# Decay products padded from 64 to 128 rows, and a new matmul price in the planner, in a two-block fp32 model kernel

## The chip, the cores and the metric

The kernel runs on one core of one Trainium2 chip. The metric is device time in microseconds (us) of one execution; before the change the median of three runs is 2162.2 us (2161.71 to 2162.23).

## What is computed

The kernel carries 512 tokens of 1024 features, in float32, through two blocks. The first one has a short convolution mixer, a gated feed-forward layer, a sparse attention mixer with compressed keys, and a second feed-forward layer. The second one runs a state-space mixer (16 heads) and a stick-breaking attention mixer (16 heads) side by side, sums both through one output projection and ends with a feed-forward layer. The change touches the state-space mixer, of which this is what matters:

```python
a_cs = jnp.cumsum(a_dt, axis=-1)            # within chunks of 128 tokens, per head
seg = a_cs[..., :, None] - a_cs[..., None, :]
decay = jnp.exp(jnp.where(causal, seg, -jnp.inf))
scores = jnp.einsum("bclgn,bcsgn->bcgls", cm, bm)
y_diag = jnp.einsum("bcgls,bcgels,bcsgep->bclgep", scores, decay, xg)
...
y_off = jnp.einsum("bclgn,bcgepn,bcgel->bclgep", cm, prev_states, jnp.exp(a_cs))
```

## The kernel before, in words

Activations lie feature-major, 128 features by 512 tokens in a tile. A float32 operand is split into a high and a low part of the type fp32r (`hilo`, `split`), and a product is three matmuls, high by high, low by high, high by low (`mm3`), summed in a PSUM bank of 128 x 512. Weights stream from HBM in groups of eight 128 x 128 blocks (`raw`); ScalarE casts a group to its high part `wh`, VectorE subtracts to get `wl`, and two split groups are held at a time (`prep`, `blk`). Tiles are named by use in the profile: `d` is the PSUM tile of any projection, `xh`/`xl`, `hb`, `hidh`/`hidl`, `ysh`/`ysl` are split activations, `qk` the token-major queries, keys and values, `lg` and `bt` the logits and log weights of a stick-breaking head, `so` its output, `ks` its stacked keys.

The program is written in stages: `layer_a` (with its feed-forward), `nsa` (compression, sparse attention, feed-forward), `block2`. In `block2` and in `nsa` independent streams are interleaved by `weave`, each with a start and an end on a common scale.

None of this is issued at once. A `Recorder` takes down every instruction, prices it and lists what it depends on (`add`, `cost`, lines 240 to 270). `arrange` then runs a list scheduler over the whole program: `forward` (L327) gives each engine, at each step, the instruction that can start first by the planner's clock, ties going to the one whose latest start, found by `backward` (L295), is earliest; for VectorE, ScalarE and GpSimd a more urgent instruction that is ready a little later can go first. Transfers on SyncE's queue are taken by program order. Some instructions may run on one of several engines (`any`), and the scheduler picks one. The result is an order of instructions for each engine and a place for each tile; the hardware then runs each queue in that order, behind semaphores. `emit` (L478) issues them, so in the profile nearly every instruction has the line L485, and tiles tell them apart.

The planner's price of a TensorE instruction stands at lines 252 to 256:

```python
passes = 1 if ins[-1].dtype == F32R else 2 if method == "transpose" else 6
o.dur = size(outs[0]) * passes / 2.4 + 3.0
o.load = (int(ins[0].ap.shape[-1]) if method == "matmul" else 128) / 1.2
```

`o.load` is the least distance to the start of the product before it (`begin`, L378). A VectorE instruction on n columns costs n * 1.042 + 68 ns, with additions for a scalar per partition and a lower rate for plain copies (L262).

The decay product is in `weights`, inside `ssd_pair` (L1373 to L1385). `ssd_prep` (L1263) puts the transposed running sums of the 16 heads into `at`, 64 rows by 512 tokens: the high part in rows 0 to 15, the low part in rows 32 to 47, zeros elsewhere (L1329 to L1332). `er` (L741) is a 64 x 16 matrix of ones at rows h and 32 + h of column h, made in `setup` from the constants, whose rows 64 to 127 are zero (L82). For each head one matmul with column h of `er`, repeated 128 times, as its weights spreads the sum of that head over all 128 partitions (L1376):

```python
mm(al, self.er[:, hd:hd + 1].to_broadcast([64, 128]), self.at, start=True, stop=True)
```

From `al`, ScalarE takes an exponential (`e`) and VectorE four differences (`dec`), from which the decay matrix of the head follows. There are 8 pairs of heads and so 16 such matmuls; the matmuls around them in PE's queue belong to other streams and have 128 rows.

Of the kernel before, what the change touches and what calls it, by code (L numbers as in the profile page):

```python
# [6 lines left out]
F32R = mybir.dt.float32r  # L7
# [79 lines left out]
def weave(*streams):  # L87
    """emits instruction streams side by side: (generator, the total of what it yields, start, end)"""
    live = [[float(st[2] if len(st) > 2 else 0), i, st] for i, st in enumerate(streams)]
    while live:  # L90
        s = min(live)
        g, total = s[2][:2]
        a, b = s[2][2:] if len(s[2]) > 2 else (0.0, 1.0)
        try:
            s[0] += (b - a) * next(g) / total
        except StopIteration:
            live.remove(s)
# [12 lines left out]
class View:  # L110
    """an access pattern of a tile that gets its place when the instructions are ordered"""
# [21 lines left out]
class Slot:  # L133
    """one tile as the program sees it, from its first access to its last"""
# [21 lines left out]
class Recorder:  # L156
    """records the instructions of the program, orders those of every engine by the time at which their
    operands are there and by their place in the program, and gives the tiles their places"""
# [8 lines left out]
    # from the end on one engine to the start on another  # L167
# [27 lines left out]
    def any(self, *ways):  # L195
        """one instruction that several engines can do, the usual one first: (engine, method, arguments)"""
        for i, (eng, method, a, *k) in enumerate(ways):
            k = k[0] if k else {}
            if i == 0:
                self.add(eng, method, a, k)  # L200
                continue
            x = Op()
            x.eng, x.call = eng, (method, a, k)
            self.cost(x, method, a, k, [a[0]], [v for v in a[1:] if isinstance(v, View)])
            self.ops[-1].ways[eng] = x.dur, x.call
# [36 lines left out]
    def cost(self, o, method, a, k, outs, ins):  # L242
        """nanoseconds on the engine, and those of a transfer"""
        size = lambda v: int(np.prod(v.ap.shape[1:]))
        n = max([size(v) for v in ins + outs[:1]])
        psum = any(v.t.psum for v in ins)
        # a scalar per partition
        one = any(isinstance(x, View) and size(x) == 1 for x in (k.values() if o.eng == "scalar" else a[2:]))
        o.move = 0.0
        if "dma" in method:  # L250
            o.dur, o.move = 1038.0 if o.eng == "gpsimd" else 475.0, size((outs + ins)[0]) * 128 * 4 / 360.0
        elif o.eng == "tensor":
            passes = 1 if ins[-1].dtype == F32R else 2 if method == "transpose" else 6
            o.dur = size(outs[0]) * passes / 2.4 + 3.0
            # the next product waits until its own matrix is loaded
            o.load = (int(ins[0].ap.shape[-1]) if method == "matmul" else 128) / 1.2
        elif o.eng == "scalar":
            o.dur = n / 1.2 + (51 if psum else 93) + (93 if one else 0) + (93 if "accum_out" in k else 0)
            o.tab = self.TABLES.get(a[2]) if method == "activation" else None
        elif o.eng == "vector":  # L260
            fast = not psum and method in ("tensor_copy", "tensor_scalar")
            o.dur = n * (6.26 if method == "reciprocal" else 0.52 if fast else 1.042) + 68 + (61 if one else 0)  # L262
        else:
            o.dur = n / 1.2 + 36
            if method == "affine_select":
                o.dur = n * 1.91
            elif method != "memset":
                o.dur = n / 1.2 + 160 + (84 if one else 0) + (n * 1.25 if method == "tensor_tensor" else 0)

    def place(self, ap):  # L270
        """the pattern on the place its tile got"""
        if not isinstance(ap, View):
            return ap
        t = ap.t
        home = t.real if t.real is not None else self.make(t, t.place)
        x = bass.AP(home.tensor, ap.ap.offset, ap.ap.ap)
        return x if x.dtype == ap.dtype else x.bitcast(ap.dtype)
# [17 lines left out]
    def backward(self):  # L295
        """the latest starts, from the end of the program"""
# [30 lines left out]
    def forward(self, urgent, look, timed=False):  # L327
# [26 lines left out]
        def avail(t):  # L354
            """when the tile can have a place, or None"""
# [15 lines left out]
        def begin(e, i, limit):  # L371
            """when the engine can start the instruction, or None if not by the limit"""
# [14 lines left out]
            if e in other:  # L387
                # one engine at a time reads a bank
                for t in o.banks:
                    at = max(at, t.read.get(other[e], -1e9) + self.LAG[other[e]][e])  # L390
            if e != o.eng:
                # another engine has to be done with it earlier than the usual one
# [8 lines left out]
        while first < len(ops):  # L401
            best = None
            for e, lst in cand.items():
# [10 lines left out]
                if top is not None and timed and e in self.PATIENT:  # L414
                    # a more urgent one that is ready soon goes first if that makes the later of the two less late
# [74 lines left out]
class Body:  # L490
# [26 lines left out]
    def alike(*views):  # L517
        """whether the Pool engine can do it: in SBUF, on the same partitions, of a size that is worth it"""
# [22 lines left out]
    def copy(self, out, a, scale=None):  # L541
        """a, by a factor"""
# [21 lines left out]
    def load(self, g, parts=None):  # L564
        """starts the transfer of a group of weight blocks"""
# [59 lines left out]
    def dense_g(self, name, n, x, ks=None, m=128):  # L625
        """the same as dense, in steps"""
# [7 lines left out]
    def dense_seq(self, specs, x, ks=None, first=2, late=1):  # L634
        """yields the finished PSUM tile of every (name, n); the late operands are used last in the first tiles,
        or every operand in all of them before the next one"""
# [10 lines left out]
    def dense_halves(self, specs, x, ks=None):  # L647
        """the same for the halves of the tokens, the first halves of all tiles before the second ones"""
# [12 lines left out]
    def dense_late(self, specs, x, first):  # L661
        """dense_seq where the second halves of the tokens come later: the first tiles take them last"""
        out = [self.ps("d") for _ in range(first)]
        for h, sl in enumerate(HALVES):
            for (name, n), p in zip(specs, out):
                # one accumulation group per bank: its first write clears the bank's flags
                self.half(p[:, sl], name, n, x, range(len(x)), sl, h == 0, h == 1)
# [5 lines left out]
    def rsq(self, src, scale, eps):  # L673
        """rsqrt(scale * src + eps) by logarithm and exponential, and a step of Newton"""
# [10 lines left out]
    def allsum(self, acc):  # L685
        """the sums over the partitions, on all of them"""
# [35 lines left out]
    def setup(self):  # L722
# [18 lines left out]
        self.er = self.nc.tile([64, 16], F32R, "er")  # L741
        nc.vector.tensor_copy(self.er, self.cst[0:64, C_E:C_E + 16])
# [71 lines left out]
    def ffn(self, x, rinv, name, gate, after, ada=False, early=0, late=0):  # L814
        """early: the first tiles take the second halves of the tokens last; late: the last tiles in halves"""
# [34 lines left out]
    def dense_out(self, name, x, late, ks=None, **kw):  # L850
        """the tiles of a product with the residual's rows, the last ones in halves: (n, PSUM, columns)"""
# [10 lines left out]
    def nsa(self):  # L862
# [39 lines left out]
        # gates token-major  # L902
# [50 lines left out]
    def stack(self, r, par, name="qs"):  # L953
        """[hi; lo] of one half of the rows, hi in its own rows"""
# [63 lines left out]
    def nsa_group(self, g):  # L1018
        """operands of one group of heads: stacked queries, doubled keys, distances, compressed values"""
# [143 lines left out]
    def block2(self):  # L1163
        nc = self.nc
        self.cols2()
        # final norm of the first block and the first norm of the second
        hb = [[self.pg(F32R, "hb") for _ in range(2)] for _ in range(ND)]
        for sl in HALVES:
            ss = self.allsum(self.acc[:, sl])
            q = self.allsum(self.acc2[:, sl])  # L1170
            # r1 * rsqrt(r1^2 q / D + e2) = rsqrt(q / D + e2 / r1^2)
# [53 lines left out]
    def share(self, name, ys, half):  # L1225
        """what half of the rows of the output projection add"""
# [7 lines left out]
    def cols2(self):  # L1234
        """per-feature factors of the two modulated norms"""
# [15 lines left out]
    def conv(self, p, j, u):  # L1251
        """causal depthwise convolution and bias of one tile of xBC"""
# [10 lines left out]
    def ssd_prep(self, hb):  # L1263
# [33 lines left out]
        # softplus: max(x, 0) + log(1 + e), e = exp(-|x|), the logarithm corrected for the rounding of 1 + e  # L1297
# [31 lines left out]
        self.at = self.pg(F32R, "at")[0:64]  # L1329
# [24 lines left out]
    def ssd_pair(self, i):  # L1354
# [18 lines left out]
        def weights(h):  # L1373
            hd = 2 * i + h
            al = self.ps("al")
            mm(al, self.er[:, hd:hd + 1].to_broadcast([64, 128]), self.at, start=True, stop=True)  # L1376
# [21 lines left out]
        # states at the end of the chunks  # L1398
# [39 lines left out]
    def sb_qk(self, nm, i, hb):  # L1438
        """queries, keys (normed over each head) or values of two pairs of heads, token-major"""
        nc = self.nc  # L1440
        p = [self.ps("qk") for _ in range(2)]
        for k in range(ND):
            w = self.blk(nm, k, i, n=2)
            for t in range(4):
                o = p[t // 2][:, 256 * (t % 2):256 * (t % 2) + 256]
                x = [y[:, 128 * t:128 * t + 128] for y in hb[k]]
                # one accumulation group per bank: its first write clears the bank's flags
# [10 lines left out]
    def sb_qk2(self, hb):  # L1458
        """the same for the first two pairs, the first halves of the tokens of queries and keys before the second ones"""
# [69 lines left out]
    # one head of the stick-breaking mixer: key tile -> (unit, column), as [keys, queries]  # L1529
# [11 lines left out]
    def sb_logits(self, hd):  # L1541
        """softplus of the logits where the key lies before the query, in two parts"""
# [16 lines left out]
    def sb_out(self, hd):  # L1559
# [12 lines left out]
        for u in (2, 0, 1):  # L1572
            w = sum(n for _, _, n in self.UNITS[u])
            b = self.ps("bt")
            # log weight: logit - (sum of the softplus terms from this key to the query)
# [28 lines left out]
    def strict(self, ap):  # L1604
        """keeps the entries whose key lies before the query"""
# [4 lines left out]
def _prepare(inputs):  # L1610
    """lays the inputs out: one matrix per name of the block stream, one array of per-partition columns"""
# [96 lines left out]
```

## Time and profile before

| | |
|---|---|
| median of 3 runs | 2162.2 us |
| span of the profiled execution, first to last instruction | 2159.8 us |
| TensorE products (PE) | 2117.5 us busy, 98% of the span, 11113 products |
| weight loads (PEld, beside PE) | 1789.1 us, 83% |
| VectorE (DVE) | 1386.1 us, 64% |
| ScalarE (ACT) | 941.8 us, 44% |
| GpSimd (POOL) | 425.9 us, 20% |
| HBM traffic | 98 GB/s over the span |

The profiled execution's own time is not listed apart from the three runs; its span is 2159.8 us, 2.4 us below their median, and that difference lies ahead of the first and behind the last instruction.

How to read it: the span runs from the first to the last instruction. A row of the timeline gives the start in us, the duration in us, engine, line, operation, the tile that is written and those that are read, and after x how many equal instructions are merged; in brackets stands the idle time of the engine ahead of it and what ended it. Records of successive matmuls overlap, since they are pipelined, so the time that a matmul takes from PE is the distance to the start of the next. The granted clock (PEclk) is 1.00 for 2.4 GHz and 0.50 for 1.2 GHz.

### The profile page before, as it was taken

Reading aid. Unit: us, or ns where it says so; the run is one execution under the profiler, and the core shown is the slowest. Engines: PE = TensorE matmul, PEld = TensorE weight load, DVE = VectorE, ACT = ScalarE, POOL = GpSimd, SP = SyncE. Lnnn points to the kernel's source line nnn. Section 1 sums busy time; section 2 is a strip of 40 time slices with the busy share of each in tenths; the row PEclk is TensorE's granted clock in tenths of the full one; section 3 lists DMA queues with packets and bytes.
Section 4 is the critical chain, followed back from the end, with each engine's and each line's share of the span. In section 5 each row is a group of like instructions: output and inputs, shape, how many; then the busy total and the mean of one; then the engine's idle time right before and its main releaser. Section 6 shows DMA issues by size and latency. Waiting matters only on the chain.

```text
span 2159.8 us, 28829 instructions
## 1 busy us (share of the span) xinstructions
PE 2117.5 (98%) x11113; PEld 1789.1 (83%) x11113; DVE 1386.1 (64%) x2347; ACT 941.8 (44%) x1587; POOL 425.9 (20%) x558
## 2 busy tenths in 40 slices
PE   8999999999999999999999999999999998999999
PEld 7888888888788777888888887989897888888887
DVE  6578754644868996654355598787879867333333
ACT  4233322332335885322222477677667746222221
POOL 1023320211223763000000141221315222000000
PEclk9999999999999999999999999999999999999999
DMA  4245652533332000222222332111121124222222
GB/s 166 98 178 188 212 183 97 175 117 104 104 127 72 1 1 31 97 98 98 98 98 98 117 127 79 59 50 59 59 69 40 40 95 140 98 98 98 98 98 98
DMA packets 60682, 214.04 MB, mean 99 GB/s; under 512 B 7424, under 2 KB 7552, under 8 KB 60544
## 3 DMA queue, kind: packets, MB, share of 16 engines
q1 hardware_dynamic: 52704, 186.50, 24.9%
q0 software_dynamic: 7840, 25.70, 3.5%
q8 instruction: 87, 1.43, 0.3%
q14 instruction: 51, 0.42, 0.1%
HBM read 210.07 MB, written 2.10 MB: 98 GB/s over the span
## 4 chain that ended last, share of the span: by engine, by line
PE 86%; DVE 9%; ACT 2%; issue 2%; POOL 1%; DMA 0%; SPq 0%; DVEq 0%; ACTq 0%; POOLq 0%
PE d L485 71%; PE qk L485 5%; PE bt L485 2%; PE o L485 2%; DVE wl L485 1%; PE so L485 1%; PE pt L485 1%; PE s L485 1%; DVE pr L485 1%; PE lg L485 1%; DVE e L485 1%; DVE ptl L485 1%; ACT wh L485 1%; DVE ss L485 0%; PE chid L485 0%
## 5 line engine op out<-in xcount | busy, mean ns | idle before, releaser
L485 ACT CAST wh<-raw 128x1024 fp32r<-128x1024 f32 (+1 forms) x332 | 347.6, 1048 | 873.1 <-PE d L485 736.8
L485 DVE TENSOR_TENSOR wl<-raw,wh 128x1024 fp32r<-128x1024 f32 (+1 forms) x342 | 424.6, 1242 | 417.3 <-ACT wh L485 414.5
L485 PE MATMUL d<-xh,wh 128*128 128x512 f32 (+1 forms) x1064 | 417.4, 394 | 6.0 <-ACT xh L485 6.0
L485 PE MATMUL d<-xh,wl 128*128 128x512 f32 (+1 forms) x1064 | 416.5, 392 | 1.0 <-DVE wl L485 1.0
L485 PE MATMUL d<-xl,wh 128*128 128x512 f32 x1064 | 416.3, 391 | 0.0
L485 PE MATMUL d<-hb,wh 128*128 128x512 f32 (+1 forms) x1136 | 332.7, 377 | 3.6 <-ACT hb L485 3.3
L485 PEld LDWEIGHTS d<-xh,wh 128*128 128x128 f32 (+1 forms) x1064 | 200.5, 189 | 47.6 <-ACT xh L485 6.0
L485 PEld LDWEIGHTS d<-hb,wh 128*128 128x128 f32 x1136 | 205.5, 190 | 40.1 <-ACT hb L485 3.5
L485 PEld LDWEIGHTS d<-xh,wl 128*128 128x128 f32 (+1 forms) x1064 | 200.3, 188 | 43.7 <-DVE wl L485 1.8
L485 PEld LDWEIGHTS d<-xl,wh 128*128 128x128 f32 x1064 | 200.4, 188 | 41.6 <-issue 0.7
L485 PE MATMUL d<-hb,wl 128*128 128x512 f32 (+2 forms) x568 | 212.3, 376 | 2.5 <-DVE wl L485 2.5
L485 PE MATMUL d<-hidh,wl 128*128 128x512 f32 (+1 forms) x561 | 211.8, 378 | 0.0
L485 PE MATMUL d<-hidh,wh 128*128 128x512 f32 (+1 forms) x561 | 211.5, 377 | 0.0
L485 PE MATMUL d<-hidl,wh 128*128 128x512 f32 (+1 forms) x561 | 211.5, 377 | 0.0
L485 PE MATMUL qk<-wh,hb 128*128 128x256 f32 x768 | 145.0, 288 | 2.1 <-ACT hb L485 1.0
L485 POOL TENSOR_TENSOR acc<-acc,sq 128x512 f32<-128x512 f32 (+1 forms) x24 | 38.2, 1591 | 499.7 <-ACT sq L485 441.9
L485 PEld LDWEIGHTS qk<-wh,hb 128*128 128x128 f32 x768 | 121.8, 193 | 6.5 <-DVE hb L485 1.5
L485 PEld LDWEIGHTS d<-hb,wl 128*128 128x128 f32 (+1 forms) x568 | 107.3, 190 | 22.6 <-DVE wl L485 3.5
L485 PEld LDWEIGHTS d<-hidl,wh 128*128 128x128 f32 x561 | 105.6, 188 | 19.4
L485 PEld LDWEIGHTS d<-hidh,wh 128*128 128x128 f32 x561 | 105.6, 188 | 19.3
L485 PEld LDWEIGHTS d<-hidh,wl 128*128 128x128 f32 x561 | 105.6, 188 | 19.2
L485 PE MATMUL qk<-wl,hb 128*128 128x256 f32 x384 | 109.0, 286 | 1.5 <-DVE wl L485 1.5
(370 smaller groups left out, 3678.5 us busy)
## 6 DMA issues: line engine op xcount, KB each, us to landing
raw<-in_wall_dram SPq DMA_DIRECT2D x345, 512.0 KB, 3.2
ada<-in_wada_dram POOLq DMA_DIRECT2D x96, 256.0 KB, 4.6
res<-in_x_dram SPq DMA_DIRECT2D x8, 256.0 KB, 7.3
out_dram<-res SPq DMA_DIRECT2D x8, 256.0 KB, 2.0
raw<-in_wall_dram SPq DMA_DIRECT2D x2, 256.0 KB, 3.7
cond<-in_c_dram POOLq DMA_DIRECT2D x2, 256.0 KB, 5.3
cst<-in_consts_dram SPq DMA_DIRECT2D x1, 394.5 KB, 7.0
mst<-in_consts_dram SPq DMA_DIRECT2D x1, 320.0 KB, 3.8
```

Source lines behind the costliest of these rows:

```text
L485: r = getattr(getattr(self.real, o.eng), m)(*[self.place(x) for x in a], **{n: self.place(x) for n, x in k.items()})
```

## The change

Two edits change what runs. The decay product gets 128 rows: `er` and `at` have 128 rows, the added ones zero. And the planner's price of a TensorE instruction changes from columns/2.4 + 3 ns to columns x 17/16/2.4 + 1 ns, with 3 ns more in the distance that a weight load imposes. No other constant of the planner and none of the weave's is changed. Everything else in the diff takes out docstrings and comments.

```diff
@@ class Recorder @@
     MARGIN = 704.3
-    # from the end on one engine to the start on another
+    COLUMN = 17 / 16 / 2.4
+
     LAG = {
@@ def cost @@
         elif o.eng == "tensor":
             passes = 1 if ins[-1].dtype == F32R else 2 if method == "transpose" else 6
-            o.dur = size(outs[0]) * passes / 2.4 + 3.0
-            # the next product waits until its own matrix is loaded
-            o.load = (int(ins[0].ap.shape[-1]) if method == "matmul" else 128) / 1.2
+            o.dur = size(outs[0]) * passes * self.COLUMN + 1.0
+
+            o.load = (int(ins[0].ap.shape[-1]) if method == "matmul" else 128) / 1.2 + 3.0
@@ def setup @@
-        self.er = self.nc.tile([64, 16], F32R, "er")
-        nc.vector.tensor_copy(self.er, self.cst[0:64, C_E:C_E + 16])
+        self.er = self.nc.tile([128, 16], F32R, "er")
+        nc.vector.tensor_copy(self.er, self.cst[:, C_E:C_E + 16])
@@ def ssd_prep @@
-        self.at = self.pg(F32R, "at")[0:64]
+        self.at = self.pg(F32R, "at")
         nc.vector.memset(self.at.bitcast(F32), 0.0)
@@ def weights, in ssd_pair @@
-            mm(al, self.er[:, hd:hd + 1].to_broadcast([64, 128]), self.at, start=True, stop=True)
+            mm(al, self.er[:, hd:hd + 1].to_broadcast([128, 128]), self.at, start=True, stop=True)
```

## Rows read from the trace of the kernel before

**Rows 1.** The page: span, and busy time of each engine.

```profile
span 2159.8 us, 28829 instructions
...
PE 2117.5 (98%) x11113; PEld 1789.1 (83%) x11113; DVE 1386.1 (64%) x2347; ACT 941.8 (44%) x1587; POOL 425.9 (20%) x558
```

**Rows 2.** Windows by stage: length, each engine's busy us (products), clock, DMA share, GB/s.

```profile
40.00:560.00 520.00, 520.00 (x2292) 430.13 (x2292) 310.42 (x479) 148.06 (x173) 108.11 (x139) 1.00 0.42 147
560.00:600.00 40.00, 34.99 (x168) 28.79 (x167) 38.58 (x51) 15.54 (x19) 15.53 (x12) 0.96 0.36 120
...
680.00:840.00 160.00, 153.92 (x1041) 124.05 (x1040) 151.18 (x504) 131.75 (x401) 101.92 (x161) 1.00 0.02 8
...
1320.00:1760.00 440.00, 431.79 (x2908) 385.35 (x2906) 354.15 (x585) 307.90 (x528) 120.28 (x155) 1.00 0.17 57
```

**Rows 3.** The page's groups: ScalarE's weight casts and the idle time ahead of them.

```profile
L485 ACT CAST wh<-raw 128x1024 fp32r<-128x1024 f32 (+1 forms) x332 | 347.6, 1048 | 873.1 <-PE d L485 736.8
```

**Rows 4.** Window of a dense stretch, instructions of tile d alone.

```profile
100.00:500.00 400.00, 399.70 (x1763) 330.69 (x1762) 48.16 (x70) 0.00 (x0) 1.00 0.47 162
```

**Rows 5.** Timeline of PE around one decay product.

```profile
1421.10 0.40 PE L485 MATMUL d<-hb,wl 128*128 128x512 f32 x1
1421.42 0.49 PE L485 MATMUL al<-at,er 64*128 64x512 f32 x1
1421.85 0.44 PE L485 MATMUL lg<-qh,ks 128*128 128x384 f32 x1
1422.12 0.34 PE L485 MATMUL lg<-ql,ks 128*128 128x384 f32 x1
1422.30 0.23 PE L485 MATMUL lg<-qh,ks 128*128 128x128 f32 x1
```

**Rows 6.** Timeline of the weight loads at the same place.

```profile
1421.42 0.18 PEld L485 LDWEIGHTS al<-at,er 64*128 64x128 f32 x1 [0.36 <-DVE wl L485]
1421.84 0.19 PEld L485 LDWEIGHTS lg<-qh,ks 128*128 128x128 f32 x1 [0.24 <-issue]
```

**Rows 7.** Timeline of PE around the sparse attention's gate transposes.

```profile
641.48 0.40 PE L485 MATMUL d<-xh,wh 128*128 128x512 f32 x1
641.81 0.46 PE L485 MATMUL gt<-cst,gr 64*128 64x64 f32 x4
642.20 0.49 PE L485 MATMUL d<-xl,wh 128*128 128x512 f32 x1
642.53 0.39 PE L485 MATMUL d<-xh,wl 128*128 128x512 f32 x1
```

**Rows 8.** Tile al: ns least/median/most, first and last start, form.

```profile
L485 PE MATMUL al<-at,er x16: 491/497/498, 1334.9 to 1697.1; 64*128 64x512 f32 x16
```

**Rows 9.** Tile at: its memset.

```profile
L485 DVE MEMSET at<- x1: 485/485/485, 1266.4 to 1266.4; 64x512 f32 x1
```

**Rows 10.** Timeline of PE in a stretch of 256-column products.

```profile
1810.47 0.40 PE L485 MATMUL d<-hb,wh 128*128 128x256 f32 x2
1810.71 0.28 PE L485 MATMUL d<-hb,wl 128*128 128x256 f32 x1
```

**Rows 11.** Timeline of DVE, two equal instructions and the next one.

```profile
562.50 1.29 DVE L485 TENSOR_TENSOR cx<-craw,vecs 128x512 f32<-128x512 f32 x2
563.70 1.63 DVE L485 TENSOR_TENSOR wl<-raw,wh 128x1024 fp32r<-128x1024 f32 x1
```

**Rows 12.** Timeline of the weight loads: the longest wait of the woven stage.

```profile
1653.26 0.19 PEld L485 LDWEIGHTS bt<-qh,ks 128*128 128x128 f32 x1 [2.41 <-DVE ks L485]
```

**Rows 13.** Timeline of DVE during that wait.

```profile
1649.96 1.46 DVE L485 CAST pvh<-pv 128x384 fp32r<-128x384 f32 x1
1651.46 0.96 DVE L485 TENSOR_TENSOR pvl<-pv,pvh 128x384 fp32r<-128x384 f32 x1
1652.45 0.76 DVE L485 SCALAR_TENSOR_TENSOR ks<-tq,vecs,ks 64x512 fp32r<-64x512 f32 x1
```

**Rows 14.** Windows of that wait and of the stretch behind it.

```profile
1650.50:1659.20 8.70, 4.95 (x36) 4.09 (x34) 8.50 (x12) 4.66 (x9) 5.67 (x6) 1.00 0.16 62
1659.20:1662.60 3.40, 3.14 (x8) 2.58 (x9) 3.37 (x7) 2.70 (x6) 0.59 (x1) 0.50 0.00 0
```

## The prediction, made before the changed kernel was run

> **What bounds the kernel now.** I read the page's busy times first: the tensor engine (PE) works in 2117.5 of 2159.8 us [rows 1]. A time is therefore changed by what PE is handed, by how fast it takes it, or by its 42.3 us of idle time, and by nothing else for long. Then I split the span by stage [rows 2]. The reader is to see two kinds of stage. In the feed-forward and projection stretches (40 to 560 us is the longest) PE is busy 520.00 of 520.00 us, while VectorE (DVE) has 310 us of work. The weight casts wait for PE and not the other way round: ScalarE sat idle for 873.1 us in front of them, 736.8 of it until a product was done [rows 3]. The mixed stages have gaps: PE idles 5.0 us in 560 to 600 (compression), 6.1 us in 680 to 840 (the sparse attention, where DVE is busy 151.2 of 160 us) and 8.2 us in 1320 to 1760 (state space and stick-breaking woven together). That is 19.3 of the 42.3 us; the rest lies at both ends of the program and in two handovers around 1250 and 1785 us, where a norm must be finished before a projection can begin. Third, I read single products: what does one cost in its place?
>
> **Part one: 128 rows in place of 64 in the decay product.** Busy time hides the answer, since records overlap; the distance from one start to the next is the price. In 100 to 500 us the `d` products alone number 1763 in 400 us [rows 4], so a 512-column product costs 400/1763 = 0.227 us. Around one decay product `al` [rows 5] the starts are 1421.10, 1421.42, 1421.85, 1422.12, 1422.30. The product ahead of it takes 0.32 instead of 0.227, the decay product 0.43 instead of 0.227, the 384-column one behind it 0.27 instead of the 0.18 of its twin. The sum is 0.09 + 0.20 + 0.09 = 0.38 us of PE time that no column needed. The weight-load rows show how: `al`'s own load starts at 1421.42, together with its own product, and the next one at 1421.84, together with the product that it serves [rows 5, 6]; nothing is loaded under the product before. So at each of the two borders the array runs empty and a weight load lies open.
>
> Is it the 64 rows, or the stretched weights (one column of `er` repeated 128 times)? The four gate transposes at 641.81 us [rows 7] have 64 rows too and ordinary weights: the product ahead takes 0.33, the one behind 0.33. The border costs the same without the stretched operand, so I put it down to the rows. With 128 rows the borders go: 16 products [rows 8] x 0.38 = 6.1 us. What is added is free or nearly so. The memset of `at` (485 ns, once, on DVE) and the set-up's cast of `er` get more partitions and no more columns; if partitions did cost, twice the memset is 0.5 us, and its first reader comes 68 us later [rows 8, 9]. The 128-row weight load lies under the product ahead, like those of the `d` products. Bounds: at the low end only the product's own excess, 16 x 0.20 = 3.2 us, if the neighbours lose for another reason; at the high end 0.33 - 0.227 = 0.10 at either border, 16 x 0.40 = 6.4 us. I take 6.1, since the gate rows show both borders. It lies on the path: PE idles 8.2 of 440 us in that stage, so about 2% of it can vanish in front of a wait.
>
> Two pages of the Trainium skill differ on whether rows can matter. The Trainium skill, "TensorE: Matmul & The Clock Gate", section "Why this matters for your kernels", says that a lone product over 32 rows takes as long as one over 128; by that the padding is worth 0 and the sum below would be the plan's term alone. The Trainium skill, "TensorEngine Tiling (Array Packing)", section "Tiling Modes", says that a change of tiling mode drains the engine; the rows agree with this one, for 64-row products between 128-row ones.
>
> **Part two: the planner's price of a product.** No instruction is added or removed; the order on every engine's queue and the places of tiles are chosen anew. The old price of a 512-column product is 512/2.4 + 3 = 216 ns, the new one 512 x 17/16/2.4 + 1 = 228 ns; the trace says 227 [rows 4]. For 256 columns it is 110 before and 114 after; the trace has two such products in 0.24 us, 120 each [rows 10]. Are the other engines priced to the same scale? Two DVE instructions fill 562.50 to 563.70, 0.60 us each [rows 11]; the planner's 512 x 1.042 + 68 is 602 ns. So PE alone ran 5% too quick in the plan, and the edit puts the engines on one scale. In the old plan PE reaches each product too early, finds its operand not yet there, and is given something that is ready in place of what is urgent; the new plan does less of that.
>
> What can it be worth? In the dense stages nothing: PE has no gap, the casts there run ahead of it [rows 2, 3], and if that cover shrank, the casts' 873 us of slack would go first. SP's weight transfers keep the program's order and are released by the casts, so they follow PE. What is open is the idle time of the stages where the planner has a choice, 5.0 + 6.1 + 8.2 = 19.3 us: the outer bound of a gain. The two handovers are chains of norms which a new order hardly shortens. For a single misordering the trace has a price. At 1650.7 us PE stands still for `ks`, its weight load idle 2.41 us [rows 12], because DVE has `pvh` and `pvl` of the state ahead of `ks` [rows 13]; a second pair of waits follows, and then the granted clock is 0.50 for 3.4 us, the 1.2 GHz level, which costs half of that. PE lost 8.70 - 4.95 = 3.75 us idle in the one stretch, and 0.26 idle and some 1.6 slow in the other [rows 14]: 5.6 us in all. New stalls of that kind are the bound on the other side; there are 8 pairs of heads, each with its own `ks` and `pv`, so several could come. I take a gain of 2 us: about that one long wait resolved, without its consequences, and everything else as often up as down. It is the least certain term.
>
> **Sum.** -6.1 - 2 = -8.1 us. The span goes from 2159.8 to about 2151.7; what lies around it (2162.2 - 2159.8 = 2.4 us against the median of the runs, which agree within 0.6) stays. Forecast: 2154 us, with 2150 to 2158 as its own range (the padding certain within 1, the plan within 3).
>
> **Rivals.**
> - *The new order makes two more waits like that for `ks`* (slower). Place: 1320 to 1760 us, where DVE is busy 354 of 440 us and where `pv`, `ks`, `dec` and `wl` compete for it. The planner now takes PE to come later, so it may leave DVE work that PE needs until later. Price 5.6 each: -6.1 + 11.2 = +5.1, so 2167 us. One such wait cancels the padding; from the second on the kernel is slower. For: DVE is the engine that the 2.41 us wait was for. Against: the scale is now right.
> - *One such wait* (no change): -6.1 + 5.6 = -0.5, about 2161.5 us.
> - *The new order also clears what is there now*: the whole 5.6 us at 1650 and half of the 6.1 us in the sparse attention, -6.1 - 5.6 - 3 = -14.7, so 2147.5 us. For: that wait is plainly a question of order. Against: at 680 to 840 DVE is nearly full, and order does not empty it.
> - *The padding does nothing*: the borders come from the stretched weights and not from the rows; then 2162.2 - 2 = 2160 us, no change. Against it stand the gate transposes [rows 7]. It is also what the first of the two pages named above would have.
>
> **How the numbers follow.** About 0.2%, 4.3 us, is what a measurement of this kernel can tell from no change; the borders are 2157.9 and 2166.5. Forecast 0.46 and the better plan 0.16 are faster: 0.62. One wait 0.18 and the idle padding 0.05 are no change: 0.23. Two waits or more: slower, 0.15. The range is 2145 to 2168: it takes in the better plan with some room, one wait, and the middle of the two-wait case, and leaves out about 0.1 above and 0.05 below.
>
> **What would show it.** In the changed trace `al` should read 128*128, its weight load should start with the product before it, and the distances around it should be 0.23, 0.23 and 0.18. If its record shortens but the distances stay, the padding rival holds. For the plan: PE's idle time in the three mixed stages against 5.0, 6.1 and 8.2 us, the stretches at half clock, and the longest of PE's waits. I am wrong if 1320 to 1760 us does not lose 4 us of length, or if the idle time of the mixed stages grows by more than the padding gives.

## The result, and the profile after

The changed kernel takes 2173.4 us (median of 4 runs, 2172.67 to 2174.9) against 2161.95 us before, measured beside it: ratio 1.0055, 95% interval 1.0041 to 1.007. It is 11.5 us slower, where 8 us faster was forecast. In every round of runs the kernel before was measured again, at 2161.8 to 2163.0 us, so times of different rounds compare within about 1 us. One execution of a later kernel ran at a granted clock of 0.751; it is left out of the times, and its profile is not read.

The page of the changed kernel, its span and the busy time of each engine (against [rows 1]):

```profile
span 2171.6 us, 28794 instructions
...
PE 2118.4 (98%) x11113; PEld 1790.2 (82%) x11113; DVE 1411.2 (65%) x2364; ACT 949.5 (44%) x1591; POOL 407.4 (19%) x537
```

PE has the same 11113 products and about the same busy time; its idle time went from 42.3 to 2171.6 - 2118.4 = 53.2 us. POOL has 21 instructions fewer, DVE 17 and ACT 4 more: the planner gave some of POOL's work to them, which the prediction did not consider. The prediction's own sign of being wrong is there: in its three mixed stages (the windows of [rows 2]) PE idles 6.6, 9.7 and 10.9 us in place of 5.0, 6.1 and 8.2, 7.9 us more, where the padding gives 6:

```profile
560.00:600.00 40.00, 33.43 (x160) 26.98 (x159) 39.11 (x50) 14.69 (x18) 14.49 (x11) 0.96 0.33 111
680.00:840.00 160.00, 150.27 (x982) 119.95 (x982) 152.06 (x516) 128.39 (x389) 95.66 (x151) 0.99 0.02 8
...
1320.00:1760.00 440.00, 429.07 (x2906) 384.78 (x2906) 365.71 (x604) 317.88 (x539) 102.43 (x141) 1.00 0.17 58
```

Did the padding work? Tile `al` of the changed kernel, in the columns of [rows 8]:

```profile
L486 PE MATMUL al<-at,er x16: 388/397/442, 1350.7 to 1709.9; 128*128 128x512 f32 x16
```

The record is 100 ns shorter, but the record is not the price; the distances are read in the first experiment, where the order is the old one. The fixed windows above hold other work in the other order. To compare the same work, I cut the span at landmarks that both orders have: the first score product `s` and the last transposition `pt` of the sparse attention, the first `qk` product of the second block, and the last product of its output projection. Windows of the changed kernel between these, in the columns of [rows 2]:

```profile
653.50:846.00 192.50, 182.77 (x1169) 147.76 (x1168) 176.74 (x581) 145.27 (x435) 105.58 (x166) 0.99 0.06 20
846.00:1261.90 415.90, 411.94 (x1919) 343.67 (x1917) 217.27 (x275) 122.25 (x151) 15.73 (x17) 1.00 0.28 98
1261.90:1795.50 533.60, 517.38 (x3433) 462.73 (x3432) 439.73 (x717) 372.08 (x634) 136.56 (x174) 0.99 0.19 67
1795.50:2171.60 376.10, 365.82 (x1734) 307.97 (x1732) 152.33 (x186) 108.46 (x134) 9.11 (x9) 0.99 0.30 104
```

They are best compared with the kernel that has the padding and the old order, which is the first experiment.

### The profile page after: what moved, and what is told of

It reads as the page before. It is cut to its first block, busy times and chain, and to the rows that moved or that the text cites. A ratio compares the mean times of both kernels' runs of the same rounds, so it can differ in the third digit from the quotient of the medians.

```text
span 2171.6 us, 28794 instructions
## 1 busy us (share of the span) xinstructions
PE 2118.4 (98%) x11113; PEld 1790.2 (82%) x11113; DVE 1411.2 (65%) x2364; ACT 949.5 (44%) x1591; POOL 407.4 (19%) x537
## 4 chain that ended last, share of the span: by engine, by line
PE 85%; DVE 10%; ACT 2%; issue 2%; POOL 1%; DMA 0%; SPq 0%; DVEq 0%; POOLq 0%; ACTq 0%
PE d L486 70%; PE qk L486 5%; PE o L486 2%; PE bt L486 2%; DVE wl L486 1%; DVE pr L486 1%; PE s L486 1%; PE so L486 1%; PE pt L486 1%; POOL res L486 1%; PE lg L486 1%; DVE e L486 1%; DVE ptl L486 1%; ACT wh L486 0%; PE chid L486 0%
## 5 line engine op out<-in xcount | busy, mean ns | idle before, releaser
L486 ACT CAST wh<-raw 128x1024 fp32r<-128x1024 f32 (+1 forms) x337 | 352.8, 1048 | 838.0 <-PE d L486 725.5
L486 DVE TENSOR_TENSOR wl<-raw,wh 128x1024 fp32r<-128x1024 f32 (+1 forms) x340 | 445.7, 1311 | 411.0 <-ACT wh L486 410.0
L486 PE MATMUL d<-xh,wh 128*128 128x512 f32 x1064 | 416.6, 392 | 6.5 <-ACT xh L486 6.4
L486 PE MATMUL d<-hb,wh 128*128 128x512 f32 (+2 forms) x1136 | 332.2, 376 | 4.6 <-ACT hb L486 4.0
L486 PEld LDWEIGHTS d<-xh,wh 128*128 128x128 f32 x1064 | 200.2, 188 | 48.5 <-ACT xh L486 6.4
L486 PEld LDWEIGHTS d<-hb,wh 128*128 128x128 f32 (+1 forms) x1136 | 205.3, 190 | 41.4 <-ACT hb L486 4.2
L486 POOL TENSOR_TENSOR acc<-acc,sq 128x512 f32<-128x512 f32 (+1 forms) x21 | 32.7, 1557 | 490.7 <-ACT sq L486 468.6
```

The source lines that it names most:

```text
L486: r = getattr(getattr(self.real, o.eng), m)(*[self.place(x) for x in a], **{n: self.place(x) for n, x in k.items()})
```

## Experiments: the two edits apart

**Padding alone.**

```diff
-        self.er = self.nc.tile([64, 16], F32R, "er")
-        nc.vector.tensor_copy(self.er, self.cst[0:64, C_E:C_E + 16])
+        self.er = self.nc.tile([128, 16], F32R, "er")
+        nc.vector.tensor_copy(self.er, self.cst[:, C_E:C_E + 16])
...
-        self.at = self.pg(F32R, "at")[0:64]
+        self.at = self.pg(F32R, "at")
...
-            mm(al, self.er[:, hd:hd + 1].to_broadcast([64, 128]), self.at, start=True, stop=True)
+            mm(al, self.er[:, hd:hd + 1].to_broadcast([128, 128]), self.at, start=True, stop=True)
```

> Padding alone; every engine's order is that of the kernel before. Theory A (the 64-row border costs 0.38 to 0.40 us a product): 2162.0 - 6.2 = 2155.8 us, and the distances around al become 0.23, 0.23, 0.18. Rival (the padding only shortens records, or its gain vanishes in front of waits): 2160 to 2162 us.

Measured: 2155.9 us against 2161.8, ratio 0.9974 (0.9965 to 0.9983). That is 5.9 us, as theory A had it. Every engine's instructions come in the order of the kernel before. The same place as in [rows 5], timeline of PE with padding alone:

```profile
1420.39 0.40 PE L485 MATMUL d<-hb,wl 128*128 128x512 f32 x1
1420.62 0.40 PE L485 MATMUL al<-at,er 128*128 128x512 f32 x1
1420.86 0.34 PE L485 MATMUL lg<-qh,ks 128*128 128x384 f32 x1
1421.03 0.34 PE L485 MATMUL lg<-ql,ks 128*128 128x384 f32 x1
1421.21 0.22 PE L485 MATMUL lg<-qh,ks 128*128 128x128 f32 x1
```

and of the weight loads (against [rows 6]):

```profile
1420.39 0.19 PEld L485 LDWEIGHTS al<-at,er 128*128 128x128 f32 x1
1420.63 0.19 PEld L485 LDWEIGHTS lg<-qh,ks 128*128 128x128 f32 x1
```

The distances are now 0.23, 0.24, 0.17 and 0.18, where they were 0.32, 0.43, 0.27 and 0.18. `al`'s load starts at 1420.39 with the product before it, and the next one at 1420.63, under `al`. Both borders are gone, so it was the rows and not the stretched weights: those are still there.

**Price alone.**

```diff
-            o.dur = size(outs[0]) * passes / 2.4 + 3.0
+            o.dur = size(outs[0]) * passes * (17 / 16 / 2.4) + 1.0
...
-            o.load = (int(ins[0].ap.shape[-1]) if method == "matmul" else 128) / 1.2
+            o.load = (int(ins[0].ap.shape[-1]) if method == "matmul" else 128) / 1.2 + 3.0
```

> The planner's new price alone, 64 rows kept. If the two edits add up: 2173.4 + 6.2 = 2179.6 us, 17.6 us slower than before, with idle time of PE grown in 560 to 600, 680 to 840 and 1240 to 1320 us. Rival (the loss needs both edits, because the padded product changes the order or the place of at): 2162 us or less.

Measured: 2176.4 us, ratio 1.0072 (1.0055 to 1.0089). The loss is the price's, by itself. The two do not quite add up: under the new price's order the padding gives 2176.4 - 2173.4 = 3 us and not 6. The traces say where the rest goes. This kernel and the changed one have the same instructions in the same order on PE, DVE, ACT and POOL, but in the changed one PE does more of its work at the granted clock 0.50, the 1.2 GHz level: 24.8 us against 14.6. Half of the 10 us between them, 5 us, is lost, more than the 3 that are missing. The sparse attention of this kernel is at 1.00:

```profile
655.20:846.00 190.80, 181.13 (x1169) 146.41 (x1168) 176.42 (x581) 145.07 (x435) 105.37 (x166) 1.00 0.06 21
```

The changed kernel has three stretches at 0.50 that this kernel has not, the first of them in that stage:

```profile
796.20:799.60 3.40, 3.40 (x14) 2.83 (x13) 3.15 (x10) 2.02 (x5) 0.82 (x2) 0.50 0.00 0
...
1277.50:1280.90 3.40, 3.40 (x18) 3.40 (x17) 3.34 (x6) 3.40 (x8) 1.48 (x2) 0.51 0.43 154
1666.60:1670.00 3.40, 3.40 (x11) 2.72 (x10) 3.29 (x8) 3.32 (x6) 0.62 (x1) 0.50 0.20 78
```

In the 12 us ahead of the first of them PE stood in three waits, of 0.6, 0.4 and 0.3 us. With the price alone it stood at the same place in the same three, and the clock stayed.

With 128 rows the price costs 2173.4 - 2155.9 = 17.5 us (16.6 between the two profiled spans). From here on every kernel has 128 rows.

Where do they arise? PE's busy time with padding alone, and windows, the landmarks as above:

```profile
PE 2111.4 (98%) x11113; PEld 1789.8 (83%) x11113; DVE 1386.0 (64%) x2347; ACT 941.4 (44%) x1587; POOL 425.9 (20%) x558
...
652.10:836.30 184.20, 178.47 (x1170) 146.25 (x1169) 171.88 (x570) 144.84 (x439) 107.78 (x172) 1.00 0.07 21
836.30:1248.60 412.30, 411.26 (x1917) 343.33 (x1914) 212.64 (x271) 119.97 (x147) 15.46 (x14) 1.00 0.30 99
1248.60:1779.30 530.70, 515.75 (x3432) 462.80 (x3433) 439.12 (x712) 368.21 (x632) 156.05 (x195) 0.99 0.20 67
1779.30:2155.00 375.70, 365.67 (x1734) 308.07 (x1732) 152.02 (x186) 107.31 (x132) 11.07 (x9) 0.99 0.31 104
```

The sparse attention takes 192.5 instead of 184.2 us (+8.3), the feed-forward with the handover behind it +3.6, the woven second block +2.9, the last stage +0.4, and what lies ahead of the sparse attention +1.4. Over the whole span PE idles 9.6 us more than with padding alone (53.2 against 43.6) and is busy 7.0 us more with the same products. Of these 7.0 the clock explains 3.6, since 24.8 us of its work are at 0.50 against 17.6. In the sparse attention PE's idle time goes from 5.7 to 9.7 us, and the stretch at 796 us costs another 1.7. There DVE is the fullest engine besides PE: busy 171.9 of 184.2 us, with 12.3 idle; after, busy 176.7 and idle 15.8. So DVE is busy longer (with 581 instructions for 570) and has more holes. What it waits for there, padding alone first (us in total, times, longest):

```profile
DVE pr L485 <- PE s L485: 1.9, 4, 0.8
DVE qr L485 <- PE d L485: 1.9, 4, 0.6
DVE ptl L485 <- ACT pth L485: 1.7, 2, 1.5
```

and in the changed kernel:

```profile
DVE pr L486 <- PE s L486: 4.1, 9, 0.9
DVE ptl L486 <- ACT pth L486: 3.6, 5, 2.2
DVE qr L486 <- PE d L486: 2.4, 5, 0.7
```

The full engine stands before score products (`s`) nine times instead of four, 4.1 us in place of 1.9. That these waits, and not those of PE on DVE, are what lengthens the stage is a reading and was not tested. In the second block the wait of [rows 12] has gone, as the prediction hoped, and others have come. Waits of PE in the changed kernel, from the first `qk` product on:

```profile
PE ssp L486 <- DVE acc L486: 4.0, 1, 4.0
PE so L486 <- DVE pv L486: 2.5, 1, 2.5
...
PE lg L486 <- DVE pv L486: 1.3, 1, 1.3
```

## Experiments: engine choice or order

The new plan has moved work from POOL to DVE, and DVE is full in the sparse attention. That was the first suspect. Two kernels plan twice (`price(0)` sets the old price, `price(1)` the new one, `search` makes the plan): once with one price, after which every instruction keeps the engine it was given, and again with the other price to make the order.

```diff
+    def arrange(self):
+        self.price(0)
+        self.search()
+        for o in self.ops:
+            o.ways = {o.eng: o.ways[o.eng]}
+        self.price(1)
+        self.search()
```

> 128 rows. The planner first runs with the old price, every instruction then keeps the engine that this plan gave it, and the order is made with the new price. Theory M (the new price leaves instructions on DVE that POOL took before, and DVE is full in the sparse attention): most of the 17.5 us between 2155.9 and 2173.4 comes back, at most 2163 us, and the sparse attention takes 184 to 187 us. Theory O (the order of the queues does it, not the choice of engine): 2168 us or more, sparse attention about 192.

Measured: 2172.8 us, ratio 1.0049 (1.0032 to 1.0065). Theory M falls: with the old choice of engines the whole loss is still there. No stage was read, so the part of theory O on the sparse attention is open.

The converse has `self.price(1)` first and `self.price(0)` second:

> 128 rows. The converse: engines as the plan with the new price gave them, order made with the old price. Theory M: 2167 us or more, DVE with 2364 instructions again. Theory O: 2162 us or less.

Measured: 2160.1 us, ratio 0.9989 (0.9979 to 0.9999), as theory O had it, with DVE's 2364 instructions. The sparse attention of this kernel:

```profile
649.90:834.90 185.00, 179.47 (x1164) 144.85 (x1163) 172.08 (x579) 143.43 (x433) 105.74 (x166) 1.00 0.07 21
```

With 579 instructions there DVE is as busy as before (172.1 us) and the stage as short (185.0), so it is not the added instructions that make it long. The 4.2 us above 2155.9 are no more than the scatter that the half-nanosecond runs below show. It is the order that costs; the fewer instructions on POOL are real, and a side effect.

## Experiments: moving the price

```diff
+            o.dur = size(outs[0]) * passes * (33 / 32 / 2.4) + 1.0
```

with 33/32, 9/8 or 31/32 in place of the change's 17/16, and its `o.load`:

> 128 rows, and only about half of the price rise (columns x 33/32/2.4 + 1: 221 ns for 512 columns). Theory S (the higher price itself misleads the planner, the loss grows with it): about 2155.8 + 8.8 = 2164.6 us. Theory R (the price is one of many numbers that decide ties, the order before was a lucky one, and any other order falls somewhere else): no order by price, anything from 2160 to 2180 us, as likely above the changed kernel's 2173.4 as below.

> 128 rows, and twice the price rise (columns x 9/8/2.4 + 1: 241 ns for 512 columns). Theory S: 2155.8 + 35 = 2191 us, at least above 2180. Theory R: 2160 to 2180 us, not ordered by price.

> 128 rows, the price moved the other way (columns x 31/32/2.4 + 1: 208 ns for 512 columns against 216 before and 228 after). Theory S as a trend: below 2155.9, about 2150 us. Theory B (the order before sits at a good point, and both sides of it are worse): 2160 us or more.

Measured: 2168.2 us at half the rise (1.003, 1.0019 to 1.0041), 2194.5 at double (1.0154, 1.0139 to 1.0169), and 2175.2 at the lower price (1.0059, 1.0044 to 1.0074). Upward the loss grows with the price, as theory S says, though half the rise already brings 12.3 of the 17.5 us; downward theory S as a trend falls, since 208 ns is as bad as 228. So is the old price only a lucky point? Half a nanosecond to either side of the old and of the new one tells:

```diff
-            o.dur = size(outs[0]) * passes / 2.4 + 3.0
+            o.dur = size(outs[0]) * passes / 2.4 + 3.5
```

and + 2.5; and 1.5 and 0.5 in place of the change's 1.0.

> 128 rows, the old price plus half a nanosecond (217 ns for 512 columns, 0.2% dearer). Theory V (there is a real best price, near the old one, with a slope to both sides): 2156 us within 2. Theory D (the list scheduler answers any small change of a price with another order, and the old order was a good draw, which its neighbours are not): above 2160 us, up to 2172.

> 128 rows, the old price less half a nanosecond. Theory V: 2156 us within 2. Theory D: above 2160 us, up to 2172, and not the same as with half a nanosecond more.

> The changed kernel with half a nanosecond more per product. Theory V: 2173 us within 2. Theory D: another draw, 2160 to 2182 us; its mean with the next run and the changed kernel tells whether the new price is worse by itself or only as a draw.

> The changed kernel with half a nanosecond less per product. Theory V: 2173 us within 2. Theory D: another draw, 2160 to 2182 us.

Measured: 2159.4 and 2161.0 us by the old price, 2175.0 and 2171.2 by the new one. A nudge of 0.2% in one number reshuffles the order and moves the time by 2 to 5 us: that is the scatter of this planner. At the old price both fall outside theory V's 2 us and one of them short of theory D's 2160; at the new price both lie within theory V's 2 us. The two clusters (2155.9, 2159.4, 2161.0 and 2173.4, 2175.0, 2171.2) stay some 14 us apart.

The next four ask whether the old price was only fitted to the planner's other numbers. The lags between engines are multiplied by 1.15, or the woven streams shifted, under either price:

```diff
+    LAG = {a: {b: 1.15 * x for b, x in r.items()} for a, r in LAG.items()}
...
-N0, N1, N2, N3, N4, N5, N6 = 0.19, 0.354, 3.201, 1.52, 2.885, -0.263, 2.5
+N0, N1, N2, N3, N4, N5, N6 = 0.19, 0.354, 3.201, 1.6, 2.965, -0.2, 2.5
...
-P0, P1, P2, P3, P4, P5, P6, P7, P8, P9, P10, P11, P12, P13 = 0.01, 1.02, 0.23, -0.031, 0.72, 1.831, 0.63, 0.61, 0.05, 0.38, 0.6, 1.53, -0.648, -0.7
+P0, P1, P2, P3, P4, P5, P6, P7, P8, P9, P10, P11, P12, P13 = 0.01, 1.06, 0.27, 0.0, 0.75, 1.87, 0.67, 0.64, 0.08, 0.42, 0.64, 1.57, -0.61, -0.66
```

> 128 rows, old price, another number of the planner disturbed: every lag between engines x 1.15. Theory F (the planner's other numbers fit the old price and only it; disturb them and the old price has no advantage): 2165 to 2177 us. Theory P (the old price is the better one by itself): 2156 to 2163 us.

> The changed kernel with the same lags x 1.15. Theory F: within 5 us of the run before it, on either side. Theory P: about 14 us above that run, the distance of the two clusters measured so far (2155.9, 2159.4, 2161.0 against 2173.4, 2175.0, 2171.2).

> 128 rows, old price, the starts and ends of the woven streams shifted by 0.03 to 0.08 of a unit. Theory F: 2165 to 2177 us. Theory P: 2156 to 2163 us.

> The changed kernel with the same shifted streams. Theory F: within 5 us of the run before it, on either side. Theory P: about 14 us above that run.

Measured: 2160.0 and 2175.6 us with other lags, 2168.4 and 2178.1 with shifted streams. The positions of the streams do matter by themselves (2168.4 lies outside of what theory P allowed and inside theory F's range), but under either disturbance the new price is worse, by 15.5 and 9.6 us. Theory F falls for the price, by the lags clearly, by the streams with a smaller distance than the 14 us of theory P.

## Experiments: the price against the other engines

```diff
+        if o.eng in self.PATIENT and "dma" not in method:
+            o.dur *= 17 / 16
```

at the end of `cost`, on top of the changed kernel; `PATIENT` holds VectorE, ScalarE and GpSimd. Then for VectorE alone, and for the other two alone.

> The changed kernel, with the planner's prices of DVE, ScalarE and GpSimd also x 17/16, so that the price of a product against theirs is that of the kernel before. Theory S (the ratio of PE's price to the others decides): 2156 us within 4. Rival (a higher price of PE makes a worse plan whatever the others cost, or any other set of numbers gives some other time): 2165 us or more.

> The changed kernel, with DVE's prices alone x 17/16. Theory S-DVE (in the sparse attention PE and DVE are both nearly full, and their ratio decides for which of the two the order is made): the sparse attention falls from 192 to 184 to 186 us and the time to 2158 to 2166 us. Rival S-all (all three engines must follow): the sparse attention stays at 189 us or more, the time at 2168 us or more.

> The changed kernel, with the prices of ScalarE and GpSimd alone x 17/16. Theory S-DVE: no help, the sparse attention at 189 to 193 us, the time 2170 to 2177 us. Rival (ScalarE's or GpSimd's price is what matters): the sparse attention at 184 to 187 us.

Measured: 2161.7 us with all three (0.9996, 0.9986 to 1.0005), 2163.8 with DVE alone (1.0007, 0.9998 to 1.0016), 2174.0 with the other two (1.0055, 1.0039 to 1.0072). Of the 17.5 us, all three give back 11.7, DVE alone 9.6, the others none. (The factor 17/16 is 6.25%; a product of 512 columns became 5.2% dearer, a shorter one less, so the old ratio is met roughly.) All three land at 2161.7, between theory S (2152 to 2160) and its rival (2165 or more); the other two as theory S-DVE said. The windows from the first `s` to the last `pt` show the same. All three:

```profile
651.80:836.10 184.30, 178.52 (x1168) 146.36 (x1167) 169.91 (x572) 146.45 (x439) 106.84 (x170) 1.00 0.06 21
```

DVE alone:

```profile
652.20:839.00 186.80, 182.29 (x1176) 146.90 (x1175) 172.82 (x572) 147.99 (x442) 107.81 (x173) 1.00 0.07 21
```

ScalarE and GpSimd alone:

```profile
654.50:846.30 191.80, 182.31 (x1169) 146.52 (x1169) 177.67 (x579) 148.34 (x441) 102.23 (x164) 1.00 0.06 20
```

and the lower price of the section before:

```profile
651.10:844.70 193.60, 184.31 (x1168) 147.25 (x1167) 178.29 (x581) 144.32 (x430) 108.07 (x169) 1.00 0.06 20
```

So, by one run each, DVE's price is the one that PE's is weighed against: 186.8 us with it against 191.8 without (0.8 us above what theory S-DVE named; the time, 2163.8, lies within). The table puts the runs side by side, with the length of that window.

| kernel (128 rows) | us | sparse attention, us |
|---|---|---|
| old price | 2155.9 | 184.2 |
| old price + 0.5 / - 0.5 ns | 2159.4 / 2161.0 | 186.2 / 184.6 |
| old price, other lags / streams | 2160.0 / 2168.4 | 185.1 / 185.2 |
| old price for the order, engines by the new one | 2160.1 | 185.0 |
| new price, all three others scaled | 2161.7 | 184.3 |
| new price, DVE scaled | 2163.8 | 186.8 |
| new price (the change) | 2173.4 | 192.5 |
| new price for the order, engines by the old one | 2172.8 | not read |
| new price + 0.5 / - 0.5 ns | 2175.0 / 2171.2 | 192.3 / 189.9 |
| new price, other lags / streams | 2175.6 / 2178.1 | 191.6 / 187.3 |
| new price, ScalarE and GpSimd scaled | 2174.0 | 191.8 |
| 221 / 241 / 208 ns for 512 columns | 2168.2 / 2194.5 / 2175.2 | 190.6 / 198.7 / 193.6 |

The stage separates the two families, if narrowly: 184.2 to 186.8 us where the price of PE against DVE is about the old one, 187.3 to 198.7 where it is raised. It does not carry the whole loss: with shifted streams it differs by 2.1 us between the two prices, the time by 9.6. Scaled prices bring the time back to 2161.7 and 2163.8 and not to 2155.9; old-price kernels with some other number moved lie at 2159.4 to 2168.4, so the remaining 6 to 8 us are within what those orders lose too (3.5 to 12.5).

What stays open is why 208 ns is bad too. Neither a rule by which the planner wants the prices that hold on the chip nor one by which a cheaper PE is always better would give it. Nor is it settled how DVE's price compares with the chip: [rows 11]'s 602 ns holds there, but another form with that price reads, in the kernel before (least, median, most),

```profile
L485 DVE TENSOR_TENSOR qs<-qr,qs x16: 685/687/1689, 647.8 to 790.4; 64x512 fp32r<-64x512 f32 x16
```

and in its place, with the next instruction right behind it, 0.71 us (756.56 to 757.27):

```profile
756.56 0.69 DVE L485 TENSOR_TENSOR qs<-qr,qs 64x512 fp32r<-64x512 f32 x1
757.27 0.29 DVE L485 TENSOR_REDUCE z<-pc 128x4 f32<-128x128 f32 x1
```

That the scheduler is greedy and its other numbers stand around the old ratio is a guess that these runs do not settle. One rival was not tested: the three prices of the section before, 208 ns among them, and the scaled kernels all keep the change's 3 ns more in `o.load`, and no run moves that number alone. For the change's loss it can be a part only, since with it kept the kernel with all three others scaled comes back to within 6 us of 2155.9, and the loss grows from 12.3 to 38.6 us with the price of the columns alone; for 208 ns it may be more.

## Why the prediction was wrong

- **The padding** was right: -6.1 forecast, -5.9 measured in the old order, with the distances that were named. Its rival, the stretched weights, is out. Of the two pages of the Trainium skill named there, "TensorEngine Tiling (Array Packing)", section "Tiling Modes", is the one that this case bears out for a change of rows (0.43 us for a 64-row product between 128-row ones, 0.24 for the same product with 128 rows); a change to 64 columns shows no such border (in the kernel before, the last product of [rows 5] is followed by one of the form `128*64` after 0.06 us, which is what its 128 columns take); the other's rule holds for a lone product, which no run here has.
- **The planner's term** is the step that failed: "the edit puts the engines on one scale", and so "the new plan does less of that". Forecast -2 us, measured +17.5. One pair of DVE instructions at 0.60 us [rows 11] stood for the scale of a whole engine. What the runs showed in its place: the plan depends on the price of PE against that of DVE; raising PE's alone by 5% is no correction of a scale but a change of that ratio, and raising DVE's as well takes more than half of the loss back (9.6 us, in one run). That the new price by itself makes the slower order is shown; why the old ratio is the better one is not.
- **The place** failed with it. The slower rival put new waits into the second block, at 5.6 us each; the second block lost 2.9 us, and the largest part, 8.3 of 16.6 us, arose in the sparse attention. The prediction had noted that DVE is nearly full there, and used it only to argue that order could not help; there the order hurt most. Its price of 5.6 us counted a stretch at half clock, and that was right in kind: there are two more such stretches than with padding alone, at 1.7 us each.
- **The bound** was too small. The loss was bounded by two or three copies of one wait. A new plan reorders everything, and the half-nanosecond runs show that it moves the time by 2 to 5 us even where nothing is meant to change; the 2 us taken for the term lay below that scatter.
- **That several could come** was right in kind: the wait for `ks` went, and waits for `pv` of 2.5 and 1.3 us and one of 4.0 for `acc` came.

The padding without the new price, 2155.9 us, is faster than both kernels.

## What to carry to other kernels

A price in a list scheduler is a weight, not a measurement: setting one engine's price to the traced value while the others keep theirs changes the ratio that decides which engine is served first, and here half of the loss arose in the stage with two nearly full engines. Before such a number is moved, nudge it by a fraction of a per cent both ways to see the scatter of the planner, and take no gain for it that is below this. And separate a sure local saving from a global reordering: here the first alone would have been a gain.

## What the runs showed that was not expected

The border was forecast at 0.38 us and came out at 5.9/16 = 0.37, rather more than one and a half products of 512 columns; what a reader of records would miss is that the product's own record shows only 0.10 of it (497 against 397 ns), and the rest lies in the distances. Two kernels with the same order, the price alone with 64 and with 128 rows, lost different amounts at the half clock: about 7 us in the one and 12 in the other, though PE stood in the same waits ahead of the first stretch that only one of them has. And the spread within one form on DVE has a long tail: of the 16 equal 64x512 subtractions ten take 685 to 702 ns, five 914 to 1140 and one 1689, so a price read off one quiet pair says little about a busy stage. What the six slow ones met is not shown.
